# Nearest-neighbour upsampling by 2: the last two of eight loads in two 8 KB rows per partition instead of one 16 KB row

## The chip, the cores and the metric

The kernel runs on one core of one Trainium2 chip. The metric is the device time of one execution in microseconds. Before the change it was 199.86 us (median of 3 runs, 199.73 to 199.90). A verdict of "faster" or "slower" asks for 2%; the runs of this kernel agree within about 0.25%.

## The reference, cut to what matters

```python
batch, channels, h, w = (16, 64, 64, 64)          # float32, 16.78 MB in
result = np.zeros((batch, channels, 2 * h, 2 * w)) # 67.11 MB out
for i in range(2 * h):
    for j in range(2 * w):
        result[:, :, i, j] = x[:, :, i // 2, j // 2]
```

Every input value is written four times. There is no arithmetic.

## The kernel before

The input is seen as 65,536 rows of 64 floats (256 bytes). Eight loads of 2 MB each bring 64 consecutive rows (16 KB) to each of the 128 partitions. All eight have tiles of their own, so no load waits for anything. A step then takes 32 rows of each partition, writes each value into a tile `u` four times over (VectorE does 18 rows, ScalarE 14), and stores 4 MB. There are two `u` tiles, 16 steps, and one queue, that of the sync engine, for all loads and stores.

```python
    blocks = [64, 64, 64, 64, 64, 64, 64, 64]
    K = 32
    KV = 18
    xf = x.rearrange("b c h w -> (b c h) w")
    of = out.rearrange("b c (h hd) w -> (b c h) (hd w)", hd=s)

    def of_block(rows, first, k):
        return rows[first : first + P * k, :].rearrange("(p k) w -> p k w", p=P)
    # ... pools: xin bufs=1, uexp bufs=2
    for n, k in enumerate(blocks):
        xt = xpool.tile([P, k, W], fdt, name=f"x{n}")
        nc.sync.dma_start(out=xt[:, :, :], in_=of_block(xf, first, k))
        loaded.append((xt, first, k))
        first += P * k
    # ...
    for xt, first, k in loaded:
        for r0 in range(0, k, K):
            u = upool.tile([P, K, s, W, s], fdt, name="u")
            nc.vector.tensor_copy(out=u[:, :KV], in_=expanded(xt[:, r0 : r0 + KV, :]))
            nc.scalar.copy(out=u[:, KV:], in_=expanded(xt[:, r0 + KV : r0 + K, :]))
            nc.sync.dma_start(
                out=of_block(of, first, k)[:, r0 : r0 + K, :], in_=u[:, :, :, :, :]
            )
```

Not shown: a helper moves the first load ahead of the barrier at the program's start. The change rewrites the helper to take a count, which stays 1.

## Time and profile before

| what | value | view |
|---|---|---|
| time, median of 3 | 199.86 us | timed runs |
| span of the profiled run | 198.0 us | page, head |
| DMA queue's share of 16 engines | 99.0% | page, part 3 |
| bytes moved, rate | 83.89 MB, 424 GB/s | page, part 3 |
| 16 KB load run | 611 ns median | packet records |
| 32 KB store run | 1,213 ns median | packet records |

A run here is a stretch of contiguous bytes that is moved as one piece; in this kernel the profile records one packet for each (1,024 of 16,384 bytes, 2,048 of 32,768 bytes).

Lines from the profile page of the kernel before. DVE is VectorE, ACT is ScalarE, SP is the sync engine, L83 is line 83 of the kernel, and a `q` after an engine's name means its sequencer, which waits and issues. Part 2 has one digit per fortieth of the span (busy tenths). A group line in part 5 gives count, total busy us, mean ns of one, then the engine's idle time before them and what ended it. Part 6 ends with the median us from issue to landing.

```profile
span 198.0 us, 149 instructions
## 1 busy us (share of the span) xinstructions
DVE 40.9 (21%) x16; ACT 52.0 (26%) x17; POOL 0.2 (0%) x4
...
DMA  8999999999999999999999999999999999999995
...
q1 hardware_dynamic: 3456, 83.89, 99.0%
...
DMA out_dram<-u 73%; ACT u L83 14%; DMA x<-in_x_dram 4%; ACTq L83 0%
...
L83 ACT COPY u<-x 128x3584 f32<-128x3584 f32 x16 | 50.8, 3179 | 128.3 <-DMA out_dram<-u 122.5
...
out_dram<-u SPq DMA_DIRECT2D x16, 4096.0 KB, 16.1
x<-in_x_dram SPq DMA_DIRECT2D x8, 2048.0 KB, 22.9
```

The DMA row is full in every slice but the first and last, while the two copying engines are idle three quarters of the time. The DMA engines are the bottleneck, and the copying engines wait for them.

Lines from the chain of waits of the same run (start us, length us, what), two steps of its steady part:

```profile
61.77 3.19 ACT u L83
64.96 0.02 issue
64.98 16.07 DMA out_dram<-u
81.05 0.02 issue
...
81.14 3.19 ACT u L83
84.33 0.02 issue
84.35 16.05 DMA out_dram<-u
```

A period of the chain is 81.14 - 61.77 = 19.37 us for two stores (two tiles `u` take turns), 9.68 us each. One store needs 9.68 us of the DMA engines but takes 16.07 from issue to landing: it stands 6.4 us in the queue behind the store before it. So the 3.19 us of ACT in the chain are not time in which the DMA engines are idle. The chain names ACT because it follows one tile, and another tile's store is always moving.

### The profile page before, as it was taken

What the parts mean: (1) busy time and instruction counts of PE and PEld (TensorE: products, weight loads), DVE (VectorE), ACT (ScalarE), POOL (GpSimd) and SP (SyncE); (2) the same over time, 40 slices, a digit from 0 to 9 for tenths busy, and PEclk for the clock granted to TensorE, in tenths of its full rate; (3) what the DMA queues carried; (4) which work ended last, traced back from release to release, by engine and by line L of the source; (5) the groups of instructions that cost most, each with busy time, mean ns of one, the idle gap of its engine ahead of it and who ended that gap; (6) DMA issues with size and microseconds to landing.
All of it is one profiled execution on the core that took longest, in us unless ns stands there. A gap on an engine that the chain in (4) does not pass through costs nothing.

```text
span 198.0 us, 149 instructions
## 1 busy us (share of the span) xinstructions
DVE 40.9 (21%) x16; ACT 52.0 (26%) x17; POOL 0.2 (0%) x4
## 2 busy tenths in 40 slices
DVE  0460000000405050505050505050505050504000
ACT  2480000000415150606060606060606060605000
POOL 0000000000000000000000000000000000000000
DMA  8999999999999999999999999999999999999995
GB/s 268 434 434 434 430 427 430 424 427 424 424 424 437 444 463 430 437 430 430 424 424 424 424 437 444 457 437 430 437 430 424 424 424 424 437 437 463 437 430 232
DMA packets 3456, 83.89 MB, mean 424 GB/s; under 512 B 384, under 2 KB 384, under 8 KB 384
## 3 DMA queue, kind: packets, MB, share of 16 engines
q1 hardware_dynamic: 3456, 83.89, 99.0%
HBM read 16.78 MB, written 67.11 MB: 424 GB/s over the span
## 4 chain that ended last, share of the span: by engine, by line
DMA 77%; ACT 14%; issue 0%; ACTq 0%
DMA out_dram<-u 73%; ACT u L83 14%; DMA x<-in_x_dram 4%; ACTq L83 0%
## 5 line engine op out<-in xcount | busy, mean ns | idle before, releaser
L83 ACT COPY u<-x 128x3584 f32<-128x3584 f32 x16 | 50.8, 3179 | 128.3 <-DMA out_dram<-u 122.5
L80 DVE COPY u<-x 128x4608 f32<-128x4608 f32 x16 | 40.9, 2560 | 139.7 <-DMA out_dram<-u 131.8
L83 ACT ACT_TABLE_LOAD x1 | 1.3, 1283 | 0.8 <-PEq L106 0.8
L106 POOL MEMSET const-bfloat16-1.0<- 128x1 bf16 x1 | 0.1, 102 | 0.0
L106 POOL MEMSET const-uint8-127<- 128x1 uint8 x1 | 0.1, 102 | 0.0
L106 POOL MEMSET const-float32-0.0<- 128x1 f32 x1 | 0.1, 98 | 0.2 <-issue 0.2
L106 POOL MEMSET const-float32-1.0<- 128x1 f32 x1 | 0.1, 98 | 0.0
## 6 DMA issues: line engine op xcount, KB each, us to landing
out_dram<-u SPq DMA_DIRECT2D x16, 4096.0 KB, 16.1
x<-in_x_dram SPq DMA_DIRECT2D x8, 2048.0 KB, 22.9
```

The costliest lines, as they stand in the source:

```text
L80: nc.vector.tensor_copy(out=u[:, :KV], in_=expanded(xt[:, r0 : r0 + KV, :]))
L83: nc.scalar.copy(out=u[:, KV:], in_=expanded(xt[:, r0 + KV : r0 + K, :]))
L106: nc = _bacc.Bacc("TRN2", target_bir_lowering=False, num_devices=1)
```

## The change

The intent is to load the last quarter of the input in the form of the stores: each of the last two loads brings two sub-blocks of 128 x 32 rows, so a partition gets two runs of 8 KB, 1 MB apart, and each of the last four stores becomes one contiguous 4 MB piece of DRAM instead of 32 KB runs at a pitch of 64 KB.

```diff
-    blocks = [64, 64, 64, 64, 64, 64, 64, 64]
+    blocks = [(1, 64), (1, 64), (1, 64), (1, 64), (1, 64), (1, 64), (2, 32), (2, 32)]
 ...
-    for n, k in enumerate(blocks):
-        xt = xpool.tile([P, k, W], fdt, name=f"x{n}")
-        nc.sync.dma_start(out=xt[:, :, :], in_=of_block(xf, first, k))
-        loaded.append((xt, first, k))
-        first += P * k
+    for n, (j, m) in enumerate(blocks):
+        xt = xpool.tile([P, j, m, W], fdt, name=f"x{n}")
+        src = xf[first : first + j * P * m, :].rearrange(
+            "(j p m) w -> p j (m w)", j=j, p=P
+        )
+        nc.sync.dma_start(out=xt[:, :, :, :], in_=src)
+        for jj in range(j):
+            parts.append((xt[:, jj], first + jj * P * m, m))
+        first += j * P * m
 ...
-    for xt, first, k in loaded:
-        for r0 in range(0, k, K):
+    for xp, first, m in parts:
+        dst = of[first : first + P * m, :].rearrange("(p m) w -> p m w", p=P)
+        for r0 in range(0, m, K):
 ...  (copies and stores as before, from xp and into dst)
```

The instruction streams of all engines and their waits are the same before and after, but for the shape of the last two loads and the addresses of the last four stores.

More of the change, by code (lines that the diff above doesn't have):

```diff
@@ L6 @@
 from concourse._compat import with_exitstack
+EARLY = 1
 def begin_before_barrier(nc):
@@ L15, in begin_before_barrier @@
     sp = mybir.EngineType.SP
-    load = next(i for i in body.instructions if i.engine == sp)
-    assert isinstance(load, mybir.InstDMACopy), type(load)
-    assert not (load.sync_info and load.sync_info.on_wait)
-    body.instructions = [i for i in body.instructions if i is not load]
+    loads = [i for i in body.instructions if i.engine == sp][:EARLY]
+    for load in loads:
+        assert isinstance(load, mybir.InstDMACopy), type(load)
+        assert not (load.sync_info and load.sync_info.on_wait)
+    names = [i.name for i in loads]
+    body.instructions = [i for i in body.instructions if i.name not in names]
     kept = list(main.instructions)
@@ L25, in begin_before_barrier @@
     )
-    kept.insert(at, load)
+    kept[at:at] = loads
     main.instructions = kept
@@ L44 @@
     fdt = x.dtype
-    blocks = [64, 64, 64, 64, 64, 64, 64, 64]
+    blocks = [(1, 64), (1, 64), (1, 64), (1, 64), (1, 64), (1, 64), (2, 32), (2, 32)]
     K = 32
-    assert P * sum(blocks) == R
+    assert P * sum(j * m for j, m in blocks) == R
     KV = 18
@@ L56 @@
     of = out.rearrange("b c (h hd) w -> (b c h) (hd w)", hd=s)
-    def of_block(rows, first, k):
-        return rows[first : first + P * k, :].rearrange("(p k) w -> p k w", p=P)
     xpool = ctx.enter_context(tc.tile_pool(name="xin", bufs=1))
     upool = ctx.enter_context(tc.tile_pool(name="uexp", bufs=2))
-    loaded = []
+    parts = []
     first = 0
-    for n, k in enumerate(blocks):
-        xt = xpool.tile([P, k, W], fdt, name=f"x{n}")
-        nc.sync.dma_start(out=xt[:, :, :], in_=of_block(xf, first, k))
-        loaded.append((xt, first, k))
-        first += P * k
+    for n, (j, m) in enumerate(blocks):
[7 more added lines that the diff above has]
+        first += j * P * m
     def expanded(rows):
@@ L75, in expanded @@
         )
-    for xt, first, k in loaded:
-        for r0 in range(0, k, K):
+    for xp, first, m in parts:
+        dst = of[first : first + P * m, :].rearrange("(p m) w -> p m w", p=P)
+        for r0 in range(0, m, K):
             u = upool.tile([P, K, s, W, s], fdt, name="u")
             nc.vector.tensor_copy(
-                out=u[:, :KV], in_=expanded(xt[:, r0 : r0 + KV, :])
+                out=u[:, :KV], in_=expanded(xp[:, r0 : r0 + KV, :])
             )
             nc.scalar.copy(
-                out=u[:, KV:], in_=expanded(xt[:, r0 + KV : r0 + K, :])
+                out=u[:, KV:], in_=expanded(xp[:, r0 + KV : r0 + K, :])
             )
             nc.sync.dma_start(
-                out=of_block(of, first, k)[:, r0 : r0 + K, :],
-                in_=u[:, :, :, :, :],
+                out=dst[:, r0 : r0 + K, :], in_=u[:, :, :, :, :]
             )
```

## The prediction

> **What bounds the kernel now.** The DMA engines. The profile page gives span 198.0 us, the one DMA queue busy 99.0% of 16 engines' span, 83.89 MB at a mean of 424 GB/s, DVE busy 21%, ACT 26%. The chain of waits is 77% DMA and 14% ACT, but the ACT part is not exposed: the timeline shows that a copy pair (3.18 us on ACT, 2.56 us on DVE) runs when one of the two output buffers comes free, while the other buffer's store is still being moved. A store takes 16.1 us from issue to landing, and buffers come free about every 9.7 us, so a store is queued about 6.4 us before the engines need it. All eight loads are issued by 4.3 us, ahead of the first store (11.05 us), and land by about 42 us; stores follow in the same queue.
>
> The packet records of the trace show the saturation: 1,024 load packets of 16,384 bytes, median 611 ns, and 2,048 store packets of 32,768 bytes, median 1,213 ns. Over 16 engines the stores are 155.3 us, the loads 40.6 us (slow first packets included): 195.8 of 198.0 us.
>
> **What the change does.** The instruction streams and all waits are unchanged, except that the last two of eight loads name 128x2 runs of 8 KB in place of 128 runs of 16 KB. Nothing is removed. Bytes, DMAs, copies, buffers and order stay; the one load sent ahead of the barrier is still one. Two things move:
> 1. 256 more load packets (512 of 8 KB for 256 of 16 KB).
> 2. The last four stores become one contiguous 4 MB piece each, where they were 32 KB runs at a 64 KB pitch.
>
> **Cost of 1.** From 611 ns for 16 KB and 1,213 ns for 32 KB, a packet costs about 9 ns plus 602 ns per 16 KB (estimate from the two medians). 256 packets over 16 engines are 16 each: 16 x 9 ns = 0.14 us, on the critical path because the queue never empties. The Trainium skill, "DMA: Bandwidth & Descriptors", section "Why small descriptors are slow (HBM only)", gives a fixed overhead of about 3 cycles per packet; small at 8 KB, in agreement with 9 ns in 611. Issuing the two loads may take longer than 0.5 us each, but the sync engine then idles until 11.05 us.
>
> **Gain of 2.** Store packets are 1,213 ns from the 5th percentile to the 95th: they run at the engine's pace (27.0 GB/s each, 432 GB/s on 16) and show no waiting for the memory. The same page, "Specifications", names 435 GB/s as the fabric ceiling. A friendlier address pattern has nothing to recover: gain 0.
>
> **Predicted time.** 199.86 + 0.14 = 200.0 us, range 199.6 to 200.5 (the three runs before spread by 0.17 us). Faster by over 2%: 0.01; within 2%: 0.98; slower by over 2%: 0.01.
>
> **What would show it.** Packets rise from 3,456 to 3,712; 8 KB packets take about 310 ns; the last load lands 0.1 to 0.2 us later, and every store after it too. Store packets stay 1,213 ns, the last four stores' included; stores 16.1 us to landing; ACT still waits about 6.4 us per step; DMA share 99%.
>
> **What would make it wrong.** 8 KB packets well above 310 ns (each 10 ns adds 0.32 us): a latency per packet that 16 KB hides; two rows of a partition 1 MB apart being slower to read; stores at the 64 KB pitch costing something that packet times hide[...]; or the loads spreading over fewer than 16 engines, which would add tens of us.

## The result, and the profile after

The changed kernel took 199.87 us (median of 6 runs, 199.63 to 200.61) and the kernel before 199.88 us in its six runs. The ratio is 1.0003, with a 95% interval of 0.9984 to 1.0022: the same. Ratios here are the mean time of one kernel's fast runs over that of the other's of the same rounds, so they are not quite the ratios of the quoted medians.

The same lines of the profile page of the changed kernel:

```profile
span 197.8 us, 149 instructions
## 1 busy us (share of the span) xinstructions
DVE 40.9 (21%) x16; ACT 52.0 (26%) x17; POOL 0.2 (0%) x4
...
DMA  7999999999999999999999999999999999999995
...
q1 hardware_dynamic: 3712, 83.89, 99.0%
...
DMA out_dram<-u 73%; ACT u L92 14%; DMA x<-in_x_dram 4%; ACTq L92 0%
...
L92 ACT COPY u<-x 128x3584 f32<-128x3584 f32 x16 | 50.8, 3179 | 128.1 <-DMA out_dram<-u 122.3
...
out_dram<-u SPq DMA_DIRECT2D x16, 4096.0 KB, 16.0
x<-in_x_dram SPq DMA_DIRECT2D x8, 2048.0 KB, 22.9
```

Its chain of waits, the same two steps:

```profile
61.71 3.19 ACT u L92
64.90 0.02 issue
64.92 16.03 DMA out_dram<-u
80.94 0.02 issue
...
81.04 3.19 ACT u L92
84.23 0.02 issue
84.25 16.00 DMA out_dram<-u
```

The only line that moved by more than 0.2 us or one digit is the packet count, 3,456 to 3,712, the 256 that the prediction counted. Copies, waits and the pace of the stores are as before. The packet records give 8 KB runs a median of 313 ns and store runs 1,213 ns, as foretold. One thing had not been foretold. Lines of the store issues by tile (count, duration min/median/max in ns, then first and last start in us), first of the kernel before and then of the changed one:

```profile
L86 SPq DMA_DIRECT2D out_dram<-u x16: 332/333/348, 11.1 to 181.2; - x16
```

```profile
L95 SPq DMA_DIRECT2D out_dram<-u x16: 332/332/2914, 11.1 to 181.0; - x16
```

One store issue, the second (at 14.16 us), occupied the sync engine for 2.9 us instead of 0.33. It did no harm, since that store had to wait behind the loads until 42 us anyway.

### The profile page after: what moved, and what is told of

It reads as the page before. It is cut to its first block, busy times and chain, and to the rows that moved or that the text cites. A ratio compares the mean times of both kernels' runs of the same rounds, so it can differ in the third digit from the quotient of the medians.

```text
span 197.8 us, 149 instructions
## 1 busy us (share of the span) xinstructions
DVE 40.9 (21%) x16; ACT 52.0 (26%) x17; POOL 0.2 (0%) x4
## 2 busy tenths in 40 slices
DMA packets 3712, 83.89 MB, mean 424 GB/s; under 512 B 384, under 2 KB 384, under 8 KB 384
## 3 DMA queue, kind: packets, MB, share of 16 engines
q1 hardware_dynamic: 3712, 83.89, 99.0%
## 4 chain that ended last, share of the span: by engine, by line
DMA 77%; ACT 14%; issue 0%; ACTq 0%
DMA out_dram<-u 73%; ACT u L92 14%; DMA x<-in_x_dram 4%; ACTq L92 0%
```

## The experiments

Theory A, of the prediction: each additional run costs a fixed 9 to 11 ns on its DMA engine, and nothing else moves. Its rivals are B (the runs cost that, and the contiguous stores or the switch from loads to stores give it back) and C (the cost of a run is hidden until runs are very short). Most of these effects are near the noise, so the experiments raise the dose, take the change apart, and use the completion times that the trace records for each DMA. A completion time here (a landing) is that of the last of its 16 engines; it is read from the trace file, since no view prints it for each DMA. Loads are numbered from 0 in the text and in the table; the expectation of `rep_after` counts from 1. The first eight runs shared a chip and the kernel-before runs (nine or ten, median 199.91 us); the last four were on another chip (nine runs of before, median 199.81 us).

| kernel | first load lands, us | loads 1 to 6, us apart (mean) | last load after the one before, us | last load lands, us | mean of timed runs, us | ratio |
|---|---|---|---|---|---|---|
| before (first profile) | 7.82 | 4.89 | 5.14 | 42.31 | 199.92 | 1 |
| rep_before | 7.74 | 4.89 | 5.27 | 42.34 | one run | |
| changed (first profile) | 7.85 | 4.91 | 4.95 | 42.24 | 199.99 | 1.0003 |
| rep_after | 7.76 | 4.90 | 4.94 | 42.12 | 199.76 | 0.9994 |
| two_split | 7.85 | 4.90 | 5.08 | 42.34 | 199.94 | 1.0002 |
| mid_two | 7.87 | 4.92 | 4.88 | 42.25 | 199.78 | 0.9996 |
| last_one | 7.73 | 4.89 | 5.37 | 42.44 | 199.88 | 1.0001 |
| act_only | 7.83 | 4.90 | 5.19 | 42.41 | 199.96 | 1.0003 |
| all_contig | 7.60 | 4.97 | 4.97 | 42.38 | 199.90 | 1.0000 |
| all_split8k | 8.26 | 4.94 | 4.91 | 42.83 | 200.25 | 1.0017 |
| all_split2k | 8.54 | 5.27 | 5.24 | 45.41 | 203.01 | 1.0155 |
| all_split512 | 10.22 | 6.93 | 6.77 | 58.55 | 216.13 | 1.0811 |

The third column is the landing of load 6 less that of load 0, over six. The mean in the row of before is that of its six runs beside the changed kernel. The two runs with 4 MB loads are told below. In every one of these runs the first store lands 9.68 to 9.73 us after the last load, and stores follow at 9.67 to 9.68 us, so a shift in the last column of landings is a shift of the end.

### rep_after: the changed kernel again

No edit.

> The changed kernel once more, unaltered. Theory A (a packet costs a fixed 9 to 11 ns, nothing else moves): 0.14 to 0.18 us longer than before, ratio 1.0007 to 1.0009, which the interval will not separate from 1; in the profile load 7 (the first of 8 KB runs) lands 4.98 us after load 6, against 4.89 between loads of 16 KB runs. Rival B (the packets cost that, and the contiguous stores or the switch from loads to stores give it back): ratio 1.0000, and the gap between the landings of the last load and of the load before it is again 4.95 us, 0.2 us shorter than the 5.14 of before. The second store's issue took 2.91 us on the sync engine in the first profile; if that is a full queue and no accident it comes again.

Measured: 199.75 us median (199.64 to 199.99), ratio 0.9994, interval 0.9980 to 1.0007. That leaves +0.14 us at the very edge. The first load of 8 KB runs took 4.96 us after the one before it, near the 4.98 of A. The last load took 4.94 us after the one before it, and the second store's issue took 2.90 us, so both features of the first trace come again. Taken alone this favours B; the later runs decide between its two givers.

### two_split: the packet part alone

```diff
-        xt = xpool.tile([P, k, W], fdt, name=f"x{n}")
-        nc.sync.dma_start(out=xt[:, :, :], in_=of_block(xf, first, k))
+        if n in (6, 7):
+            G = 32
+            xt = xpool.tile([P, k // G, G * W + 16], fdt, name=f"x{n}")
+            nc.sync.dma_start(out=xt[:, :, : G * W], in_=xf[first : first + P * k, :]
+                .rearrange("(p g m) w -> p g (m w)", p=P, m=G))
```

> The packet part of the change alone: the last two loads are cut into two 8 KB runs per partition by a 64 byte gap in the tile, and all addresses in DRAM, so all stores too, stay as in the kernel before. A: as the change itself, +0.14 to 0.18 us, ratio about 1.0008. B with contiguous stores as the giver: the full +0.18 us and every store landing that much later than in the changed kernel.

Measured: 199.91 us median, ratio 1.0002, interval 0.9989 to 1.0014. Its mean is 0.02 us over that of before and 0.18 over the changed kernel's in the same rounds, with overlapping runs (199.84 to 200.09 against 199.64 to 199.99). Its last store lands at 197.24 us, 0.2 us later than in the two traces of the changed kernel (197.03 and 197.06), as B expected; but the difference arises in the last load (5.08 us against 4.95 and 4.94), before any store with a changed address. This alone settles nothing; the next two have four times the dose.

### all_contig: the change on all eight loads

```diff
-    blocks = [(1, 64), (1, 64), (1, 64), (1, 64), (1, 64), (1, 64), (2, 32), (2, 32)]
+    blocks = [(2, 32)] * 8
```

> The change on all eight loads: 1,024 more packets, 64 an engine, and all 16 stores contiguous. A: 64 x 9 to 11 ns = 0.58 to 0.70 us longer, ratio 1.0029 to 1.0035, last load landing at about 43.0 us against 42.3. B: four times the gain too, so ratio 1.000 again, with the last load late but stores landing at less than 9.68 us spacing.

Measured: 199.89 us median (199.81 to 199.98), ratio 1.0000, interval 0.9987 to 1.0012. The 1.0029 of theory A lies outside. This is the clearest result against A at this size: 64 additional runs per engine lengthen the whole by at most 0.0012 x 199.9 = 0.24 us by the interval, under 4 ns each.

In the middle of the load phase the 8 KB runs are slower, and by what A says. The row is a stretch of time, busy time of the engines in it, then the DMA share and GB/s; first of the kernel before, then of this one:

```profile
10.00:40.00 30.00, 2.88 (x2) 4.11 (x2) 0.00 (x0) 1.00 1.01 428
```

```profile
10.00:40.00 30.00, 2.65 (x2) 3.88 (x2) 0.00 (x0) 1.00 1.01 424
```

Landings are 4.97 us apart instead of 4.89, which for 8 additional runs is 10 ns each. Yet the last load lands at 42.38 us, as in the kernel before (42.31 and 42.34). The lag of six such steps, 6 x 0.08 = 0.5 us, is set off at the two ends: the first load lands 0.14 to 0.22 us sooner, and the last, behind which the stores begin, takes 4.97 us here and 5.14 to 5.27 there. What lies behind these two ends is taken up after `rep_before`.

### all_split8k: the same run sizes, stores at the old addresses

The edit is that of `two_split` with `n in (0, 1, 2, 3, 4, 5, 6, 7)`.

> All eight loads in 8 KB runs by the gap in the tile, all stores at the 64 KB pitch as before. A: the same as the run with contiguous stores within 0.2 us, so 0.6 to 0.7 us over before, ratio 1.003. B: 0.6 us or more longer than the run with contiguous stores, which differs from this one in the store addresses (and the load addresses) alone.

Measured: 200.25 us median (200.12 to 200.34), ratio 1.0017, interval 1.0005 to 1.0030. Compared with `all_contig` this is 0.35 us longer with no overlap of the runs. Rival B, in its form with contiguous stores, would claim this, but the profile puts the difference elsewhere. The stores are not slower: they land 9.67 us apart on the mean, against 9.68 in `all_contig`. The difference is there when the first load lands. Lines of the chain of waits, first of `all_contig`, then of `all_split8k`; the first piece is the first copy, which waits for that load, and the last is that of the sixteenth and last step:

```profile
7.62 6.27 ACT u L92 x2
61.85 3.19 ACT u L92
...
178.06 3.18 ACT u L92
```

```profile
8.28 6.27 ACT u L99 x2
62.31 3.19 ACT u L99
...
178.38 3.18 ACT u L99
```

The lag is 0.66 us at the first copy, 0.46 at the second piece and 0.32 at the last. The issue of the first load occupied the sync engine for 627 ns against 431, so a tile with gaps seems to take longer to start; why a gap adds that, no run tells. Stores of contiguous addresses are ruled out as the giver: nothing is gained while stores run.

### all_split2k: a seven-fold dose

The edit is that of `two_split` on all loads with `G = 8`, each copy cut in two pieces of 8 rows, 16 rows on each engine.

> All eight loads in 2 KB runs by gaps in the tile (addresses in DRAM as before; each copy in two pieces, 16 rows on each engine): 448 more packets an engine. A: 448 x 9 to 11 ns = 4.0 to 4.9 us longer, 204 to 205 us, ratio 1.020 to 1.025, 2 KB packets of 85 ns. Rival C (a packet's cost hides behind the next until packets are very short, so 8 KB cost nothing and 2 KB little): under 1 us longer. The sync engine should stand in its load issues for tens of us if the queue holds a limited number of packets, at no cost in time, since stores come behind all loads anyway.

Measured: 203.02 us median, ratio 1.0155, interval 1.0139 to 1.0170. C's limit of 1 us is broken; A's size is somewhat high in the end time: (203.01 - 199.91) us / 448 = 6.9 ns a run instead of 9 to 11. The packet records have 8,192 runs of 2,048 bytes with a median of 84 ns, as A said. The load phase runs at 398 GB/s:

```profile
10.00:40.00 30.00, 3.20 (x3) 5.86 (x4) 0.00 (x0) 1.00 1.05 398
```

And the sync engine stands in its load issues, here of `all_split2k`:

```profile
L68 SPq DMA_DIRECT2D x<-in_x_dram x8: 545/5081/5153, 0.0 to 26.0; - x8
```

An issue takes 5.1 us, nearly the 5.27 us in which one load is moved: the sync engine is held to the pace of the queue. The Trainium skill, "Perfetto Trace Analysis", section "DMA Instruction — HWDGE (DVE, Sync)", says that the reported time of such an issue covers waiting for and using the descriptor generator, and that engines can begin early, particularly when more descriptors are made than their buffer holds. This trace agrees in kind: its first two load issues took 0.63 and 0.55 us, its last four 5.1 to 5.2 us. As expected it costs nothing by itself, for the DMA engines are busy throughout (the queue's share is 99.6%).

### all_split512: a thirty-fold dose

The edit is that of `two_split` on all loads with `G = 2` and a gap of 8 floats, each copy in two pieces of alternate rows.

> All eight loads in 512 byte runs: 1,984 more packets an engine. A: 1,984 x 9 to 11 ns = 17.9 to 21.8 us longer, 218 to 222 us, ratio 1.09 to 1.11, packets of 28 ns. C: more than the straight line from the 2 KB run gives, or much less.

Measured: 216.13 us median, ratio 1.0811, interval 1.0797 to 1.0826. That is (216.13 - 199.91) us / 1,984 = 8.2 ns a run; A's size is again somewhat high. It is more than the straight line from the 2 KB run (1,984 x 6.9 ns = 13.7 us), which is one of the outcomes that C named, so the end times alone do not exclude a part that is hidden. The packet times do: the medians of 2, 8, 16 and 32 KB packets (84, 309, 611 and 1,213 ns) lie within 1 ns of a straight line, 8.4 ns + 37.6 ns per KB, so a run of 8 KB bears the same fixed 8.4 ns as one of 2 KB. The form of the expectation was wrong in one point: no 28 ns packets appear. The trace records only 4,480 packets, the count of `all_split8k`, because sixteen runs of 512 bytes are recorded as one packet of 8 KB:

```profile
DMA packets 4480, 83.89 MB, mean 392 GB/s; under 512 B 384, under 2 KB 384, under 8 KB 384
```

Their median is 436 ns against 309 for an unbroken run of 8 KB, so 127 / 15 = 8.5 ns for each additional run inside the packet, and the line above gives 16 x (8.4 + 18.8) = 435 ns. The gaps also shift runs off multiples of 256 bytes in the tile, which no run varies alone; at 8 KB it shows no cost (309 ns with gaps in `all_split8k`, 311 without in `all_contig`). The count of packets in a profile is therefore not the count of runs, and the cost goes with the runs.

### wide: longer runs

```diff
-    blocks = [64, 64, 64, 64, 64, 64, 64, 64]
+    blocks = [128, 128, 128, 128]
```

> The other way: four loads of 32 KB runs, 32 packets an engine fewer than before. A: 32 x 9 to 11 ns = 0.29 to 0.35 us shorter, ratio 0.9983; the first copies start at about 12.7 us instead of 7.85, which costs nothing because the loads fill the queue until 42 us. If the late first copies do cost: the first store lands later than 51.9 us. This is the version that could beat both kernels.

Measured: 199.98 us median (199.91 to 200.03), ratio 1.0003, interval 0.9990 to 1.0017. The expected gain of 0.3 us is not there, and the interval leaves at most 0.2 us of it. The late first copies cost nothing: the first store lands at 52.01 us, against 51.99. Three loads (12 MB) had landed at 31.61 us, 0.67 us ahead of the same bytes in the kernel before, and the last took 10.71 us instead of the 9.70 of the others, to land at 42.32. The lead was lost at the end of the loads. A small part of the time, 0.25 us, is at the very end: the span ends 1.06 us after the last store's landing, 0.81 in all kernels with eight loads.

### last_one, mid_two and taper: what takes the lead back

By now the switch from loads to stores looked like the place where differences vanish: after 16 KB runs the last load took 0.25 us more, after 32 KB runs 1.0 us, and almost nothing after 8 KB runs. I called this B'.

```diff
+    blocks = [(1, 64)] * 7 + [(2, 32)]                    # last_one
+    blocks = [(1, 64)] * 2 + [(2, 32)] * 2 + [(1, 64)] * 4 # mid_two
+    blocks = [(1, 128)] * 3 + [(1, 64), (2, 32)]          # taper
```

> Only the last load in 8 KB runs (two contiguous stores). Found so far in the landings: 8 KB runs lengthen a load by 0.06 to 0.08 us, but the last load, behind which the stores start, takes 5.14 us in 16 KB runs and 4.95 in 8 KB runs, where the others take 4.89. Theory B' (the switch from loads to stores costs about 0.25 us after 16 KB runs and almost nothing after 8 KB runs): the last load lands 4.95 to 5.0 us after the one before, about 0.1 to 0.2 us shorter than before in all. Rival A (packets alone): 0.07 us longer.

Measured: 199.79 us median, ratio 1.0001, interval 0.9986 to 1.0015. The last load, in 8 KB runs, took 5.37 us. B' wanted 4.95 to 5.0, so it fails here (one trace). A's 0.07 us is within the noise (199.88 us in the mean against 199.85 of before in the same rounds).

> The change on loads 2 and 3 in place of 6 and 7: as many packets and as many contiguous stores as the change, but the last load in 16 KB runs. B': loads 2 and 3 take 4.96 us each, the last one 5.14, so 0.14 to 0.16 us longer than before and 0.2 to 0.3 longer than the change (200.05 against 199.75). If contiguous stores or chance gave it back: the same as the change, 199.75.

Measured: 199.66 us median, ratio 0.9996, interval 0.9983 to 1.0008. Loads 2 and 3 took 4.97 us each, as expected, but the last load, in 16 KB runs, took 4.88 us where B' wanted 5.14, and the time was not longer. B' fails again (one trace), and the other outcome came, the time of the changed kernel (199.78 us in the mean against 199.76 in `rep_after`, though on another chip). In this kernel no store issue took longer than 0.35 us, although it has as many 8 KB runs as the changed kernel; so the long issue of the second store does not follow from the number of runs alone.

> Three loads of 32 KB runs, one of 16 KB, then one in two 8 KB runs: 40 packets an engine fewer than before, and the small packets where the stores start. In the run with four loads of 32 KB runs the third landed at 31.61 us against 32.28 for the same bytes before, and then the last took 10.71 us in place of 9.70. B': 32.28 - 31.61 = 0.67 us kept, and 0.2 gained at the switch: the last load lands at about 41.5 us against 42.3, time 199.1 to 199.4, below both kernels though far under 2%. A: -0.3 us. If the switch cost comes with the early lead and not with the packet size: the last load lands at 42.3 us again and the time is 199.9.

Measured: 199.99 us median, ratio 1.0006, interval 0.9994 to 1.0019. Three 4 MB loads had landed at 31.69 us, and still the last of all landed at 42.30 us, after 5.71 us for its 2 MB in 8 KB runs. A's gain of 0.3 us lies outside the interval. So the third outcome came true: what was to be lost at the switch was the lead, whatever the size of the last runs. Neither this kernel nor `wide` beats the two that it was meant to beat.

> The kernel before once more, for a second profile: B' wants the last load at 5.1 to 5.2 us after the one before, the other loads 4.87 to 4.9, and no store issue longer than 0.4 us.

Measured, one run: 199.82 us. The other loads landed 4.86 to 4.90 us apart, the last 5.27 us after the one before (0.07 us over the expected range), and no store issue took longer than 0.35 us.

Together: kernels with runs of 8, 16 and 32 KB, in any mix and place, land their last load between 42.12 and 42.44 us, with the one exception of `all_split8k`, whose first load was late. Differences of up to 0.67 us midway are gone by then. The trace narrows down where.

First, it holds the completion of each of the 16 engines, not only of the last. In the mean over the 16, the last load of `all_contig` is through at 42.14 us, against 41.91, 41.75 and 41.87 in the three traces with 16 KB runs throughout (before, `rep_before`, `act_only`). So a lag of 0.2 to 0.4 us is there (one trace of `all_contig`); the landing hides it, because the slowest engine is 0.24 us behind the mean in `all_contig` and 0.40 to 0.59 in the others. The earlier first landing of `all_contig` is of the same kind: in the mean its first load is through at 7.36 us, against 7.34 to 7.41.

Second, the packet records show where a lead is lost. Load packets that start after 38 us, just before the first stores, can take up to about two and a half times their median (1,244 ns for 611 in the kernel before, 2,198 for 1,213 in `wide`, 789 for 309 in `taper`). Their time above the median, summed and divided by 16, is 0.46, 0.18 and 0.32 us in the three traces with 16 KB runs, 0.91 in `wide` and 0.73 in `taper`, but 0.04 in `all_contig` and 0.07 in `all_split8k`. The size of the last runs does not decide it (0.73 and 0.29 us after 8 KB runs in `taper` and `last_one`, 0.08 after 16 KB runs in `mid_two`). What slows these packets stays open.

### act_only: is the ACT share of the chain time that counts?

```diff
-            nc.vector.tensor_copy(out=u[:, :KV], in_=expanded(xt[:, r0 : r0 + KV, :]))
-            nc.scalar.copy(out=u[:, KV:], in_=expanded(xt[:, r0 + KV : r0 + K, :]))
+            nc.scalar.copy(out=u[:, :], in_=expanded(xt[:, r0 : r0 + K, :]))
```

> All copies on ACT, 32 rows each, none on DVE: a copy step takes 7.3 us (3.18 x 32/14) instead of 3.18. Theory (the 14% ACT in the chain is not exposed, a store is queued 6.4 us early): step plus wait is 9.7 us, so the 6.4 us of wait shrink to about 2.4 us and the time stays within 0.3 us, ratio 1.00. Rival (the chain's ACT share is time that counts): 7 steps or more lengthen by 4.1 us each, 29 us or more longer.

Measured: 199.93 us median (199.91 to 200.05), ratio 1.0003, interval 0.9988 to 1.0018. Lines from its page and then from its chain:

```profile
DMA out_dram<-u 61%; ACT u L78 28%; DMA x<-in_x_dram 4%; ACTq L78 0%
...
L78 ACT COPY u<-x 128x8192 f32<-128x8192 f32 x16 | 112.2, 7017 | 70.8 <-DMA out_dram<-u 34.6
```

```profile
61.85 7.03 ACT u L78
68.88 0.01 issue
68.89 12.25 DMA out_dram<-u
81.15 0.02 issue
...
81.22 7.03 ACT u L78
```

ACT's share of the chain doubled from 14% to 28%, and the time did not move. The period is 81.22 - 61.85 = 19.37 us, the same to the digit: the copy grew from 3.19 to 7.03 us and the store's time from issue to landing shrank from 16.07 to 12.25, because the store now stands in the queue for 2.6 us instead of 6.4. The idle time of ACT before its copies fell from 128.3 us in all to 70.8. (The 34.6 us in the line leave out one wait of 30.4 us, that for the first store, which the view puts down to "issue"; in the 122.5 us of before it is included.) The chain's share of a line is not what shortening that line would save.

## Why the prediction was right or wrong

- **The bottleneck: right, and shown.** The DMA engines set the time. `act_only` shows that copies can more than double without effect, and the two high doses show that a delay of the last load arrives in full at the end: the last load of `all_split512` lands 16.2 us late (58.55 against 42.31) and the time is 16.2 us longer.
- **The total: right.** It foretold 200.0 us, in 199.6 to 200.5; the median was 199.87. The range is over six times as wide as the 0.14 us term, so the total would have been right without the term too: it confirms that nothing large moves, not the term.
- **The counts and the run times: right.** 3,712 packets, 8 KB runs of 313 ns (about 310 foretold), store runs still 1,213 ns, stores 16.0 us to landing, DMA share 99.0%.
- **"Gain of 2" is 0: right.** `all_contig` has all 16 stores contiguous and its stores land 9.68 us apart, as with the old addresses.
- **"Cost of 1 ... 16 x 9 ns = 0.14 us, on the critical path": the failed term.** "The last load lands 0.1 to 0.2 us later" did not happen (42.24 and 42.12 us against 42.31 and 42.34; in the mean over the 16 engines 41.85 and 41.87 against 41.75 to 41.91). One dose is within the noise, so the higher doses decide: at four times the dose the expected 0.6 us were absent in `all_contig` (1.0000, at most 1.0012), and 0.34 us came in `all_split8k` (1.0017). What the runs showed in its place: the 8 KB runs do lengthen the loads in mid-stream by 0.06 to 0.08 us each, about 10 ns a run, but by the end of the load phase differences of this size are set off. At 448 and 1,984 additional runs per engine the term is real in the end time, at 6.9 and 8.2 ns a run. With 8.4 ns a run from the packet medians, the 64, 64, 448 and 1,984 additional runs of `all_contig`, `all_split8k`, `all_split2k` and `all_split512` should cost 0.5, 0.5, 3.8 and 16.7 us; they cost 0.0, 0.3, 3.1 and 16.2, so each is 0.2 to 0.7 us short, with no growth with the dose. The step that failed is therefore that the cost lies "on the critical path" in full, not the size of a run's cost. The 9 ns compared load runs of 16 KB with store runs of 32 KB, a weak footing, but they held: the 32 KB load runs of `wide` have a median of 1,213 ns too.
- **"In agreement with 9 ns": too generous.** The Trainium skill's "DMA: Bandwidth & Descriptors", section "Why small descriptors are slow (HBM only)", says 3 cycles a packet. At the 850 MHz that its "Specifications" table gives for the fabric, my estimate of that is 3.5 ns; the packet medians give 8.4 ns, and 6.9 to 8.2 ns were measured in the end time at high doses. The page gives no clock for those cycles. It agrees that the effect is small at 8 KB, not in its size.
- **Why differences vanish at the end of the loads: open.** Where they vanish is seen: in a smaller spread between the engines, and in load packets just before the first stores that take longer than their median. Contiguous stores are ruled out by the stores' pace, and the size of the last runs by `last_one`, `mid_two` and `taper`, one trace each. The whole of the open matter is worth under 0.5% of the time.

## What to carry to other kernels

With the DMA queue full from start to end and every run already 8 KB or more, the form of the runs was no lever here: going from 16 KB to 8 KB or to 32 KB moved the time by less than 0.2%, and only at 2 KB (1.6%) and 512 bytes (8%) did it count. Before working on an engine that the chain of waits names, see how long its product then stands in the queue: here 6.4 us of standing hid all 3.2 us of copying. And a lead or lag seen halfway is not yet a gain or loss: compare landings at the end of the phase, and look at the mean over the engines as well as the slowest one.

## What the Trainium skill lacked or had wrong

- "DMA: Bandwidth & Descriptors", section "Why small descriptors are slow (HBM only)": it gives about 3 cycles a packet and lets joining runs into packets remove that part, while a second part, 32 bytes of descriptor data per operation, stays. Here sixteen runs of 512 bytes were recorded as one 8 KB packet, and each additional run inside still cost 8.5 ns (436 ns against 309). At the 27 GB/s of a store run (32,768 bytes in 1,213 ns), 32 bytes are 1.2 ns, an estimate, so the part that stays does not explain it.
- The same page, section "Where 436 GB/s comes from": it says that for transfers between HBM and SBUF the per-core HBM side (about 358 GB/s) binds. With one core at work the loads ran at 428 GB/s and the stores at 4.194 MB / 9.68 us = 433 GB/s, near the 435 of the fabric. For one core alone that sentence is too low, and the page's own single-core measurement of 425 fits; no run here had two cores at work.
- "Perfetto Trace Analysis", section "DMA Instruction — HWDGE (DVE, Sync)": it tells that a descriptor buffer can fill but not how much it holds. Here the issue of a DMA grew from 0.33 to 2.9, 5.1, 6.9 and 8.7 us (second store of the changed kernel, 2 KB loads, 512 byte loads, second store of `all_contig`), and two kernels with the same number of runs differed (2.9 us in the changed kernel, 0.35 at most in `mid_two`).
- No page has the longer issue of a load into a tile with gaps: 627 ns for the first load against 383 for an unbroken 16 KB row and 431 for two 8 KB rows without a gap. A later load of two rows without a gap took up to 646 ns in `mid_two`, so only first loads are compared.
